# One weight block of the third projection taken into a decoder kernel's first rows, and an attention output computed turned, with the values as the stationary operand

## The chip, the cores and the metric

The program runs on one core of a Trainium2 chip. A core has five engines, each with its own queue of instructions: TensorE (PE, with its weight loads PEld), VectorE (DVE), ScalarE (ACT), GpSimd (POOL) and SyncE (SP). SP issues nearly all DMA transfers. The metric is the device time of one execution in microseconds (us), as the median of several runs; lower is better.

## The reference

Two decoder layers work on a sequence of 256 rows of 1024 features, all in float32. Cut to what matters:

```python
for i in range(2):
    h = rms_norm(x, norm_g[i])
    rq, rk, rv, rz, mq, mk, mv, mz = split(h @ w_in[i])      # eight groups of 512 columns
    r_out = silu(rz) * retention(rotary(rq), rotary(rk), rv, ret_norm_g[i])   # 4 heads of 128
    m_out = silu(mz) * softmax_attention(rms_norm(mq), rms_norm(mk), mv, rel_bias)   # 4 heads of 128
    x = x + concat([r_out, m_out]) @ w_out[i]
    gate = sigmoid(rms_norm(x) @ w_ple_gate[i])
    x = x + gate * rms_norm(p[i] @ w_ple[i], ple_norm_g[i])
```

With 256 rows the attention ("moba") has one block, so it is plain causal softmax attention with a bias per distance. Retention is linear attention with a decay by distance, followed by a normalisation per head.

## The kernel before

**Splitting floats.** TensorE multiplies in a reduced format (fp32r) at a quarter of the cost of full fp32 (in the profile 12 matmuls of 256 columns take 1.38 us, and 12 of 128 columns in full fp32 2.68 us). The kernel keeps full precision by splitting an operand into a high and a low part: ScalarE casts the high part, VectorE subtracts to get the low part, and three products (high x high, high x low, low x high) take the place of one. Weights come from memory through `wst` tiles (class `Stage`, 512 KB a chunk, two 128-row blocks k), are cast into `wh` (L350) and subtracted into `wl` (L353). `mm3` (L405 to L407) issues the three matmuls of 512 columns for one block k and one half m of the 256 rows. Small products are left in full fp32, which the profile shows as two records for one matmul.

**Order of the work in a layer.** The eight projections run in the order MQ, MK, RQ, RK, MZ, MV, RV, RZ (M for softmax attention, R for retention; Z are the gates). Then come the output projection, whose first half takes the softmax heads (k 4 to 7 of the tile `yT`) and whose second half takes the retention heads (k 0 to 3), the embedding product, and the gate product. Results of a projection leave PSUM through chains of operations on VectorE and ScalarE. Where a result is needed turned (features on partitions), `halves` (L621, ScalarE) sorts it into two 16-bit halves, `turned` sends it through a transposing DMA on SP's queue (L631), and VectorE copies the halves together (L640).

**First rows.** At the start nothing is on the chip. `first_rows` (L553) takes MQ's eight blocks one by one as they land; each block's transfer (`first_block`) brings 512 weight columns and 256 columns of the input. Blocks 0 and 1 of MK's weights (`key_block`, 256 KB each) lie behind blocks 0 and 1. The order in memory and on SP's queue is that of the dictionary `EARLY`.

**Attention.** `moba_scores` computes scores with query rows on partitions (L932, L950); `probs` adds the bias, takes the exponential and turns the result into the tile `PT` (keys on partitions; tile name PS in the profile). `moba_out` multiplies `PT` by the values `V` with the probabilities stationary (`pv`, L960, which retention's output uses too); `moba_y` multiplies by the gate and the reciprocal of the softmax sum (L978), turns the result and splits it into `yT` (`to_parts`, L657 and L659). Retention follows in `ret_scores_own` (L1010), `ret_scores` (L932), the decays `decayed` (L999), `ret_out` (L960), `ret_norm` and `ret_gate` (L1076). The tile `ST` of the retention scores takes the buffer of `PT`.

**What sets the order.** The program is laid out by a planner at build time (class `Flow`). Every chain of operations is a generator that asks for an engine with an estimated time, buffers to take and chains to wait for. The planner keeps a clock for each engine and gives the engine to the ready chain that is due first. What it lays down is a fixed order for each engine's queue. PE's order is that of the program text, but the small attention products stand in a list of groups, and `tick` puts one in between the matmuls of a projection once its inputs have been ready, by the planner's clock, for a margin.

Of the kernel before, what the change touches and what calls it, by code (L numbers as in the profile page):

```python
# [51 lines left out]
EARLY = {0: FIRST, "late": S, ("K", 0): GW, 1: BLOCK, ("K", 1): GW, **{k: BLOCK for k in range(2, KT)}}  # L52
# [3 lines left out]
LANES, LINE = 4, 4  # L56
TILE = 12 * ROW
HOP = 0.15
TURN = 0
AHEAD = 1.6  # L60
# [5 lines left out]
LIFT = {("gen", 38): 4.0, ("rope", 3): -7.0, ("gen", 4): -4.0, ("gate", 1): 1.0, ("hr1", 3): 2.0}  # L66
# [188 lines left out]
def tile_hybrid_trunk(ctx: ExitStack, tc: tile.TileContext, early, x, pT, ple_g, rel_bias,  # L255
# [243 lines left out]

    def key_half(src, hi, lo):  # L500
        yield ask(DVE, 0.35)
        nc.vector.tensor_copy(hi[:, S:], src[:, S:])
        firsts["K", 0, "lo"] = flow.begin(key_low(0, src, hi, lo), -19.6, flow.end + HOP)
# [52 lines left out]
    def first_blocks():  # L556
        home, at = act_p.tile([P, KT, 2, S], F32, name="a").rearrange("p k t s -> p (k t s)"), 0
        for k in range(KT):
# [6 lines left out]
            if k < 2:  # L565
                firsts["K", k] = flow.begin(key_block(k), k - 19.5, 0.0)
            at += BLOCK if k else 2 * FIRST
# [5 lines left out]
    for l in range(DEPTH):  # L573
# [3 lines left out]
        for g, half in pairs_in:  # L577
            skip = l == 0 and {MQ: 2, MK: 1 - half}.get(g, 0)
# [191 lines left out]
    def layer(l, aT):  # L770
# [92 lines left out]
        def value(g, m, ps):  # L863
            yield ask(ACT, 0.585, take=() if m else ("V",), after=need_stats(m) + ((VA[g],) if m else ()))
            if not m:
# [16 lines left out]
        def after_proj(g, m, ps):  # L882
# [4 lines left out]
            if g == RZ:  # L887
                YC[m, 0] = made(yT, m, 0, c)
# [22 lines left out]
        def probs(m, h0, per, ps):  # L911
# [16 lines left out]
            yield from turned(u, lambda: raw[:, :, h0:h0 + per, m * P:m * P + n])  # L928

        def three(ps, w, x):  # L930
            for i, (a, b) in enumerate(((0, 0), (0, 1), (1, 0))):
                nc.tensor.matmul(ps, w[a], x[b], start=i == 0, stop=i == 2)  # L932

        def moba_scores():
# [17 lines left out]
            for n in ("T", "T", "K2", "Q2"):  # L952
                flow.free(n, flow.clock[PE])

# [9 lines left out]
        yT, YC = Parts(), {}  # L964

        def moba_y(m, ps):
            ri = small(H, "ri")
            yield ask(DVE, 0.1)
# [3 lines left out]
            yield ask(DVE, 0.26, take=("tok",), after=(GC[MZ, m],))  # L972
            y = tok_p.tile([P, GW], F32, name="tok")
            for h in range(H):
                if h:
                    yield ask(DVE, 0.26)
                sl = slice(h * DH, (h + 1) * DH)
                nc.vector.scalar_tensor_tensor(y[:, sl], ps[:, sl], ri[:, h:h + 1], G[MZ][:, m, sl],  # L978
                                               op0=ALU.mult, op1=ALU.mult)
            flow.free("mix")  # L980
# [14 lines left out]
        SC, RO, RC = {}, {}, {}  # L995

        def decayed(h0, n, cols, ps):
            yield ask(DVE, 0.605, after=(L_DEC,))
# [4 lines left out]
        def ret_scores_own():  # L1003
            q, k = T[RQ], T[RK]
            flow.take("PS")
            box["ST"] = big.tile([P, H, S + P], F32, name="PS", bufs=1)
# [19 lines left out]
        def ret_norm(m, ps):  # L1026
# [23 lines left out]
            RO[m] = o  # L1050

        def ret_out():
            for m in range(MT):
                ps = pv(m, lambda h, m, b: box["ST"][:, h, S:] if b else box["ST"][:, h, m * P:(m + 1) * P], V[RV])
                RC[m] = flow.begin(ret_norm(m, ps), flow.soon(9.6))
# [257 lines left out]
```

## Time and profile before

| quantity | value |
|---|---|
| median of 3 runs | 296.58 us (296.27 to 297.05) |
| span of the profiled execution, first to last instruction | 294.1 us |
| median above that span | 2.48 us |
| PE busy | 288.9 us (98% of the span), 1411 matmul records |
| VectorE busy | 253.5 us (86%) |
| ScalarE busy | 214.7 us (73%) |
| GpSimd busy | 30.9 us (11%) |
| moved by DMA | 69.77 MB, mean 237 GB/s |

The page lists no separate whole time for the profiled execution; its span stands in the table, and the runs' times are longer by what lies around the span. The shares of busy time are averages over stages with different limits, so a change is read in its own stage. In a timeline row the columns are start, duration, engine, line, operation, output and inputs, and number of instructions; in brackets stands the engine's idle time before it and what ended it. Records of consecutive matmuls overlap, so the distance between starts is what one costs.

### The profile page before, as it was taken

To read this page: it belongs to the slowest core of one execution; us is meant where nothing else is said; L and a number is where in the kernel's file an instruction comes from. 1 tells how busy PE (TensorE), PEld (TensorE's weight loads), DVE (VectorE), ACT (ScalarE), POOL (GpSimd) and SP (SyncE) were. 2 spreads that over 40 slices of the span, in tenths; PEclk is the share of its full clock that TensorE was granted. 3 is DMA by queue.
4 is the path that set the end of the run, shared out by engine and by line. 5 is a ranking of instruction groups with operands and counts; after the bars stand their busy time and mean duration, and the time that the engine had idled before them with its cause. 6 is when DMAs were issued, how large, how long until landed. Compare 5 with 4: busy or idle time off the path is not lost.

```text
span 294.1 us, 4301 instructions
## 1 busy us (share of the span) xinstructions
PE 288.9 (98%) x1411; PEld 246.5 (84%) x1411; DVE 253.5 (86%) x461; ACT 214.7 (73%) x376; POOL 30.9 (11%) x44
## 2 busy tenths in 40 slices
PE   8999999999999999999999999999999999999994
PEld 4788888888899888888888888888898988888884
DVE  3967799999899999699999589999998797969942
ACT  3979974799747893998585896599646869479411
POOL 5004200000001200022003220000000030001300
PEclk9999999999999999999999999999999999999999
DMA  7999999998969868698689969787999766943021
GB/s 220 378 403 410 290 244 309 377 290 187 245 193 270 337 150 280 152 245 319 166 198 296 370 187 220 281 222 170 242 322 243 274 226 176 295 89 71 0 75 71
DMA packets 61774, 69.77 MB, mean 237 GB/s; under 512 B 46260, under 2 KB 47160, under 8 KB 61624
## 3 DMA queue, kind: packets, MB, share of 16 engines
q1 hardware_dynamic: 61712, 69.50, 79.7%
q8 instruction: 11, 0.18, 0.3%
q14 instruction: 11, 0.09, 0.1%
q0 software_dynamic: 32, 0.01, 0.0%
q10 hardware_dynamic: 8, 0.00, 0.0%
HBM read 57.42 MB, written 1.05 MB: 199 GB/s over the span
## 4 chain that ended last, share of the span: by engine, by line
PE 96%; DMA 2%; SPq 0%; ACT 0%; DVE 0%; issue 0%
PE acc L406 26%; PE acc L405 26%; PE acc L407 26%; PE acc L553 4%; PE mix L960 4%; PE mix L932 2%; DMA a<-in_early 2%; PE mix L407 1%; PE mix L743 1%; PE mix L742 1%; PE mix L406 1%; PE mix L744 1%; PE mix L405 1%; PE mix L1010 1%; PE mix L950 1%; ACT wh L459 0%
## 5 line engine op out<-in xcount | busy, mean ns | idle before, releaser
L405 PE MATMUL acc<-wh,a 128*128 128x512 f32 (+1 forms) x286 | 107.8, 377 | 0.0
L406 PE MATMUL acc<-wl,a 128*128 128x512 f32 (+1 forms) x286 | 107.7, 377 | 0.0
L407 PE MATMUL acc<-wh,a 128*128 128x512 f32 (+1 forms) x286 | 107.4, 376 | 0.0
L353 DVE TENSOR_TENSOR wl<-wst,wh 128x1024 fp32r<-128x1024 f32 x76 | 92.0, 1222 | 9.1 <-ACT wh L350 8.9
L350 ACT CAST wh<-wst 128x1024 fp32r<-128x1024 f32 x76 | 78.6, 1054 | 15.2 <-PE acc L407 6.0
L405 PEld LDWEIGHTS acc<-wh,a 128*128 128x128 f32 x286 | 53.5, 187 | 9.1
L407 PEld LDWEIGHTS acc<-wh,a 128*128 128x128 f32 x286 | 53.5, 187 | 9.0
L406 PEld LDWEIGHTS acc<-wl,a 128*128 128x128 f32 x286 | 53.5, 187 | 8.7
L621 ACT COPY u<-tok 128x1024 uint16<-128x1024 uint16 x30 | 31.1, 1053 | 12.7 <-DVE tok L978 7.9
L657 ACT CAST a<-tmp 128x512 fp32r<-128x512 f32 x20 | 12.4, 618 | 10.9 <-DVE tmp L654 8.3
L621 ACT COPY u<-x_t 128x1024 uint16<-128x1024 uint16 x12 | 12.5, 1042 | 10.2 <-DVE x_t L1138 6.8
L673 POOL TENSOR_TENSOR ro<-rs_t,neghalf 128x4 f32<-128x4 f32 x4 | 5.8, 1460 | 129.0 <-DVE rs_t L671 129.0
L640 DVE COPY tmp<-w 128x512 uint16<-128x512 uint16 x40 | 16.4, 466 | 0.1
L659 DVE TENSOR_TENSOR a<-tmp,a 128x512 fp32r<-128x512 f32 x20 | 13.7, 685 | 0.0
L640 DVE COPY T<-w 128x512 uint16<-128x512 uint16 x32 | 12.9, 467 | 0.7 <-DMA w<-u 0.7
L553 PE MATMUL acc<-wh,a 128*128 128x512 f32 (+1 forms) x42 | 11.3, 387 | 0.3 <-ACT wh L459 0.3
L960 PEld LDWEIGHTS mix<-V,PS 128*128 128x128 f32 x96 | 11.3, 192 | 0.3
L1189 DVE SCALAR_TENSOR_TENSOR tmp<-tmp,E 128x512 f32<-128x512 f32 (+1 forms) x9 | 5.7, 629 | 6.7 <-ACT tmp L1183 3.8
L960 PE MATMUL mix<-V,PS 128*128 128x128 f32 x96 | 11.4, 275 | 0.0
L1186 ACT ACTIVATE tmp<-acc,hr 128x512 f32<-128x512 f32 (+1 forms) x8 | 5.0, 631 | 8.5 <-PE acc L407 8.5
L405 PE MATMUL acc<-T,a 128*128 128x512 f32 (+1 forms) x30 | 11.0, 367 | 0.0
L407 PE MATMUL acc<-T,a 128*128 128x512 f32 (+1 forms) x30 | 10.9, 365 | 0.0
(144 smaller groups left out, 458.2 us busy)
## 6 DMA issues: line engine op xcount, KB each, us to landing
wst<-in_w_in SPq DMA_DIRECT2D x59, 512.0 KB, 6.3
wst<-in_w_out SPq DMA_DIRECT2D x16, 512.0 KB, 6.6
wst<-in_w_gate SPq DMA_DIRECT2D x16, 512.0 KB, 4.6
wst<-in_w_ple SPq DMA_DIRECT2D x4, 512.0 KB, 7.6
wst<-in_early SPq DMA_DIRECT2D x4, 384.0 KB, 7.4
a<-in_early SPq DMA_DIRECT2D x3, 384.0 KB, 5.8
x_t<-in_x SPq DMA_DIRECT2D x1, 1024.0 KB
gb<-in_ple_g SPq DMA_DIRECT2D x2, 512.0 KB, 6.7
```

Source lines behind the costliest of these rows:

```text
L350: nc.scalar.copy(hi, s)
L353: nc.vector.tensor_tensor(lo, s, hi.bitcast(F32), op=ALU.subtract)
L405: nc.tensor.matmul(ps, ah, wh, start=start, stop=False)
L406: nc.tensor.matmul(ps, ah, wl, start=False, stop=False)
L407: nc.tensor.matmul(ps, al, wh, start=False, stop=stop)
L553: nc.tensor.matmul(ps[m][:, sl], (a0.lo if which[0] == "lo" else a0.hi)[:, k, m * P:(m + 1) * P], columns(w, sl), start=start and i + j == ...
L621: nc.scalar.copy(u, src.bitcast(U16).rearrange("p (n t) -> p t n", t=2))
L640: nc.vector.tensor_copy(v, w[:, t].rearrange("p (h b) k -> p h (b k)", h=v.shape[1]))
L657: nc.scalar.copy(h, src)
L659: nc.vector.tensor_tensor(a.lo[:, k0:k0 + 4, m * P:(m + 1) * P], src, h.bitcast(F32), op=ALU.subtract)
L932: nc.tensor.matmul(ps, w[a], x[b], start=i == 0, stop=i == 2)
L960: nc.tensor.matmul(ps[:, h * DH:(h + 1) * DH], lhs(h, m, b), v[:, b, h * DH:(h + 1) * DH], start=b == 0, stop=b == m)
```

## The change

Two edits go together. The first takes block 0 of RQ's weights (the third projection) into the early transfers ahead of block 1, with its matmuls right after block 0 of MK, and block 1 of RQ's weights behind block 7, with its matmuls after block 6. RQ's own loop then leaves out these two blocks.

The second changes the softmax attention's output in both layers. The values are the stationary operand and the turned probabilities the moving one, so that the output comes with features on partitions. The probabilities over keys that both halves of the rows see, and the values of the first half of the keys, are split into high and low parts; for these three fp32r matmuls of 256 columns stand where one fp32 matmul per half stood. The rest (second half of the keys, second half of the rows) stays one fp32 matmul of 128 columns per head. The gate times the reciprocal is turned instead of the output (`gate_turned`), and lies in the part of `PT` that has been split already. The output is multiplied by it and split straight into `yT`. The parts of the probabilities lie in `yT`'s first half, those of the values in blocks 6 and 7 of `yT`, until `yT` is written. The retention scores take the buffer of `PT` only when the gates in it have been used, so the take stands on VectorE in `decayed`. Some planner constants change.

```diff
-EARLY = {0: FIRST, "late": S, ("K", 0): GW, 1: BLOCK, ("K", 1): GW, **{k: BLOCK for k in range(2, KT)}}
+EARLY = {0: FIRST, "late": S, ("K", 0): GW, ("R", 0): GW, 1: BLOCK, ("K", 1): GW, **{k: BLOCK for k in range(2, KT)}, ("R", 1): GW}
+THIRD = -19.3, -12.9
+GATES = 6.0
-LIFT = {("gen", 38): 4.0, ("rope", 3): -7.0, ("gen", 4): -4.0, ("gate", 1): 1.0, ("hr1", 3): 2.0}
+LIFT = {("gen", 38): 4.0, ("rope", 3): -7.0, ("gen", 4): -4.0, ("gate", 1): 1.0, ("hr1", 3): 2.0, ("rope", 2): 4.0}
...
+    def third_block(k):
+        yield ask(SP, 0.43, take=() if k else ("wst",), mb=0.25)
+        if not k:
+            firsts["R"] = wst_p.tile([P, 2, GW], F32, name="wst")
+        src = firsts["R"][:, k]
+        nc.sync.dma_start(src, early_block(("R", k)))
+        yield ask(ACT, 0.62, take=() if k else ("w",))
+        if not k:
+            firsts["Rw"] = wh_p.tile([P, 2, GW], F32R, name="wh"), wl_p.tile([P, 2, GW], F32R, name="wl")
+        hi, lo = firsts["R", k, "w"] = [v[:, k] for v in firsts["Rw"]]
+        nc.scalar.copy(hi, src)
+        firsts["R", k, "lo"] = flow.begin(key_low(k, src, hi, lo), THIRD[k] + 0.2, flow.end + HOP)
...
-            skip = l == 0 and {MQ: 2, MK: 1 - half}.get(g, 0)
+            skip = l == 0 and {MQ: 2, MK: 1 - half, RQ: 1 - half}.get(g, 0)
...
         def value(g, m, ps):
...
-            nc.scalar.activation(V[g][:, m], ps, AF.Copy, scale=stats(m)[0 if g == MV else 2])
+            if m or g == RV:
+                nc.scalar.activation(V[g][:, m], ps, AF.Copy, scale=scale)
+            else:
+                hi, lo = box["VT"] = [yT.both[:, k].rearrange("p t s -> p (t s)") for k in (6, 7)]
+                nc.scalar.activation(hi, ps, AF.Copy, scale=scale)
+                yield ask(DVE, 0.665)
+                nc.vector.scalar_tensor_tensor(lo, ps, scale, hi.bitcast(F32), op0=ALU.mult, op1=ALU.subtract)
...
         def probs(m, h0, per, ps):
...
+            src, hi, lo = (v[:, h0:h0 + per, m * P:(m + 1) * P] for v in (box["PT"], yT.hi, yT.lo))
+            yield ask(ACT, 0.1 + 0.11 * per)
+            nc.scalar.copy(hi, src)
+            yield ask(DVE, 0.08 + 0.13 * per)
+            nc.vector.tensor_tensor(lo, src, hi.bitcast(F32), op=ALU.subtract)
...
+        def turn_gates():
+            for m in range(MT):
+                if (MZ, m) in GC and (m, 2 * m) in PC and m not in GTC:
+                    GTC[m] = flow.begin(gate_turned(m), flow.soon(GATES))
+        def gate_turned(m):
             ri = small(H, "ri")
+            yield ask(DVE, 0.1, after=(GC[MZ, m], *PC.values()))
             nc.vector.reciprocal(ri, DEN[m])
             yield ask(DVE, 0.14)
             nc.vector.tensor_scalar(ri, ri, stats(m)[1], None, op0=ALU.mult)
-            yield ask(DVE, 0.26, take=("tok",), after=(GC[MZ, m],))
-            y = tok_p.tile([P, GW], F32, name="tok")
-            for h in range(H):
...
-                nc.vector.scalar_tensor_tensor(y[:, sl], ps[:, sl], ri[:, h:h + 1], G[MZ][:, m, sl],
-                                               op0=ALU.mult, op1=ALU.mult)
+            yield ask(DVE, 0.605, take=("tok",))
+            o = tok_p.tile([P, GW], F32, name="tok")
+            nc.vector.tensor_tensor(o.rearrange("p (h d) -> p h d", h=H), G[MZ][:, m].rearrange("p (h d) -> p h d", h=H),
+                                    ri[:, :, None].to_broadcast([P, H, DH]), op=ALU.mult)
...
-            u = yield from halves(y, "tok")
-            yield from to_parts(yT, m, 4, u)
+            u = yield from halves(o, "tok")
+            raw = box["PT"].bitcast(U16).rearrange("p h (k t) -> p t h k", t=2)
+            yield from turned(u, lambda: raw[:, :, :, m * P:(m + 1) * P])
+        def moba_y(i, ps):
+            yield ask(DVE, 0.605, take=("tmp",), after=tuple(GTC[m] for m in range(MT)))
+            t = tmp_p.tile([P, GW], F32, name="tmp").rearrange("p (h s) -> p h s", h=2)
+            nc.vector.tensor_tensor(t, ps.rearrange("p (h s) -> p h s", h=2), box["PT"][:, i::2, :S], op=ALU.mult)
+            flow.free("mix")
+            if i:
+                flow.free("PS")
+            yield ask(ACT, 0.53)
+            hi, lo = (v[:, H + i::2] for v in (yT.hi, yT.lo))
+            nc.scalar.copy(hi, t)
+            yield ask(DVE, 0.605)
+            nc.vector.tensor_tensor(lo, t, hi.bitcast(F32), op=ALU.subtract)
 
         def moba_out():
-            for m in range(MT):
-                ps = pv(m, lambda h, m, b: box["PT"][:, h, (m + b) * P:(m + b + 1) * P], V[MV])
-                YC[m, 4] = made(yT, m, 4, flow.begin(moba_y(m, ps), flow.soon(3.1)))
-            flow.free("PS", flow.clock[PE])
+            vh, vl = box["VT"]
+            banks = [bank(mix_p, "mix") for _ in range(2)]
+            for h0 in range(0, H, 2):
+                heads = [(h, slice(h * DH, (h + 1) * DH), banks[h - h0][:, h0 * P:h0 * P + S]) for h in range(h0, h0 + 2)]
+                for h, d, o in heads:
+                    flow.row(0.342)
+                    three(o, [v[:, d] for v in (vh, vl)], [v[:, h] for v in (yT.hi, yT.lo)], False)
+                for h, d, o in heads:
+                    flow.row(0.22)
+                    nc.tensor.matmul(o[:, P:], V[MV][:, 1, d], box["PT"][:, h, S:], start=False, stop=True)
...
         def decayed(h0, n, cols, ps):
-            yield ask(DVE, 0.605, after=(L_DEC,))
+            own = n == H
+            yield ask(DVE, 0.605, take=("PS",) if own else (), after=(L_DEC,) if own else (L_DEC, SC["own"]))
+            if own:
+                box["ST"] = big.tile([P, H, S + P], F32, name="PS", bufs=1)
...
         def ret_gate(g, m, ps):
...
-            while m not in RC:
-                yield ask(DVE, 0.0)
-            yield ask(DVE, 0.605, take=("tok",), after=(RC[m],))
+            yield ask(DVE, 0.605, take=("tok",), after=(RN[m],))
...
+            pr = [bank(mix_p, "mix") for _ in range(MT)]
             for k in range(KT):
                 first_rows(k, ps, k == 0, k == KT - 1)
                 if k < 2:
                     first_rows(k, pk, k == 0, False, ("K",))
+                if k in (0, 6):
+                    first_rows(k // 6, pr, k == 0, False, ("R",))
```

More of the change, by code (lines that the diff above doesn't have):

```diff
@@ L863, in value @@
         def value(g, m, ps):
-            yield ask(ACT, 0.585, take=() if m else ("V",), after=need_stats(m) + ((VA[g],) if m else ()))
-            if not m:
+            first = m == (g == MV)
+            yield ask(ACT, 0.585, take=("V",) if first else (),
+                      after=need_stats(m) + ((VA[g],) if m and g == RV else ()))
+            scale = stats(m)[0 if g == MV else 2]
+            if first:
                 V[g] = big.tile([P, MT, GW], F32, name="V", bufs=1)
                 flow.reach(VA[g])
-            nc.scalar.activation(V[g][:, m], ps, AF.Copy, scale=stats(m)[0 if g == MV else 2])
+            if m or g == RV:
[5 more added lines that the diff above has]
+                nc.vector.scalar_tensor_tensor(lo, ps, scale, hi.bitcast(F32), op0=ALU.mult, op1=ALU.subtract)
             flow.free("acc")
@@ L887, in after_proj @@
             if g == RZ:
-                YC[m, 0] = made(yT, m, 0, c)
+                made(yT, m, 0, c)
+            if g == MZ:
+                turn_gates()
         def project(gs, by_m=False, pre=None):
@@ L928, in probs, with three @@
             yield from turned(u, lambda: raw[:, :, h0:h0 + per, m * P:m * P + n])
-        def three(ps, w, x):
+            src, hi, lo = (v[:, h0:h0 + per, m * P:(m + 1) * P] for v in (box["PT"], yT.hi, yT.lo))
[3 more added lines that the diff above has]
+            nc.vector.tensor_tensor(lo, src, hi.bitcast(F32), op=ALU.subtract)
+        def three(ps, w, x, stop=True):
             for i, (a, b) in enumerate(((0, 0), (0, 1), (1, 0))):
-                nc.tensor.matmul(ps, w[a], x[b], start=i == 0, stop=i == 2)
+                nc.tensor.matmul(ps, w[a], x[b], start=i == 0, stop=stop and i == 2)
         def moba_scores():
@@ new lines, in gate_turned @@
+            raw = box["PT"].bitcast(U16).rearrange("p h (k t) -> p t h k", t=2)
[12 more added lines that the diff above has]
+            nc.vector.tensor_tensor(lo, t, hi.bitcast(F32), op=ALU.subtract)
+            flow.free("tmp")
@@ new lines, in moba_out @@
+        def moba_out():
+            vh, vl = box["VT"]
[8 more added lines that the diff above has]
+                    nc.tensor.matmul(o[:, P:], V[MV][:, 1, d], box["PT"][:, h, S:], start=False, stop=True)
+            for i, ps in enumerate(banks):
+                c = flow.begin(moba_y(i, ps), flow.soon(3.1))
+                for m in range(MT):
+                    for k in range(H + i, KT, 2):
+                        yT.made[m, k] = c
@@ L991, in moba_out @@
             flow.free("V", flow.clock[PE])
             ret_scores_own()
-        SC, RO, RC = {}, {}, {}
+        SC, RO, RN = {}, {}, [Mark() for _ in range(MT)]
         def decayed(h0, n, cols, ps):
-            yield ask(DVE, 0.605, after=(L_DEC,))
+            own = n == H
+            yield ask(DVE, 0.605, take=("PS",) if own else (), after=(L_DEC,) if own else (L_DEC, SC["own"]))
+            if own:
+                box["ST"] = big.tile([P, H, S + P], F32, name="PS", bufs=1)
             nc.vector.tensor_tensor(box["ST"][:, h0:h0 + n, cols], ps.rearrange("p (h t) -> p h t", h=n),
@@ L1117, in layer @@
                 load_p(l)
-            project((g,), by_m=g == RZ)
+            project((g,), by_m=g == RZ, pre={(RQ, m): pr[m] for m in range(MT)} if l == 0 and g == RQ else None)
         force_groups()
@@ L1285 @@
     early["late"] = sides[:, 1]
-    early |= {("K", k): w_in[0, MK, 0][:, k] for k in range(2)}
+    early |= {(n, k): w_in[0, g, 0][:, k] for n, g in (("K", MK), ("R", RQ)) for k in range(2)}
     w_gate = rows(a["w_ple_gate"], GW, 2)
```

18 lines of the change are left out of this document (8 added, 10 removed).

## The prediction

> **What bounds the kernel now.** I read the page's head and its chain that ended last, then TensorE's own waits, then the first ten microseconds instruction by instruction, then VectorE's share by stage.
>
> ```profile
> span 294.1 us, 4301 instructions
> PE 288.9 (98%) x1411; PEld 246.5 (84%) x1411; DVE 253.5 (86%) x461; ACT 214.7 (73%) x376; POOL 30.9 (11%) x44
> PE 96%; DMA 2%; SPq 0%; ACT 0%; DVE 0%; issue 0%
> ```
> ```profile
> PE acc L553 <- ACT wh L459: 0.3, 1, 0.3
> ```
>
> TensorE (PE) carries 96% of the chain that sets the end, and after the warm-up it has a single listed wait. A busy PE is not proof, because busy intervals overlap; so I checked the distance between starts, which a stall would stretch.
>
> ```profile
> 6.98 0.61 PE L553 MATMUL acc<-wl,a 128*128 128x512 f32 x2
> 7.92 0.72 PE L553 MATMUL acc<-wh,a 128*128 128x512 f32 x2 [0.33 <-ACT wh L459]
> 8.64 0.71 PE L553 MATMUL acc<-wl,a 128*128 128x512 f32 x2
> 9.20 1.50 PE L553 MATMUL acc<-wh,a 128*128 128x512 f32 x6
> 18.46 0.60 PE L553 MATMUL acc<-wh,a 128*128 128x512 f32 x2
> 18.91 0.38 PE L405 MATMUL acc<-wh,a 128*128 128x512 f32 x1
> ```
>
> From 9.20 to 18.91 there are 44 matmuls of 512 columns: 0.22 us each, no gap. Before 9.20 the same pitch shows what is lost: two matmuls from 6.98 should let the next start at 7.42 (it starts at 7.92, lost 0.50), two from 7.92 at 8.36 (8.64, lost 0.28), two from 8.64 at 9.08 (9.20, lost 0.12). So 0.90 us is lost around weight block 1, and from 9.20 on the kernel is a row of matmuls: the end moves by what leaves PE's work, by what fills those 0.90 us, and by any new stall.
>
> **Part one: block 0 of the third projection among the first rows.** Why PE loses time there:
>
> ```profile
> 5.52 0.29 DVE L502 CAST wh<-wst 128x256 fp32r<-128x256 f32 x1 [0.56 <-DMA wst<-in_early]
> 5.96 0.69 DVE L507 TENSOR_TENSOR wl<-wst,wh 128x512 fp32r<-128x512 f32 x1
> 7.25 0.62 ACT L459 CAST wh<-a 128x512 fp32r<-128x512 f32 x1 [1.32 <-DMA a<-in_early]
> 7.25 0.35 DVE L467 TENSOR_SCALAR a<-a 128x256 fp32r<-128x256 f32 x1 [0.59 <-DMA a<-in_early]
> 7.90 0.69 DVE L518 TENSOR_TENSOR wl<-a,wh 128x512 fp32r<-128x512 f32 x1 [0.30 <-ACT wh L459]
> 8.51 0.48 DVE L523 SCALAR_TENSOR_TENSOR a<-a 128x256 fp32r<-128x256 f32 x1
> ```
> ```profile
> 5.50:7.25 1.75, 1.75 (x9) 1.23 (x7) 0.99 (x3) 0.41 (x2) 1.44 (x5) 1.00 1.05 360
> 7.25:9.00 1.75, 1.41 (x6) 0.59 (x4) 1.45 (x4) 1.39 (x3) 0.32 (x2) 1.00 1.02 404
> ```
>
> Block 1 lands at about 7.2; ScalarE's cast, VectorE's low part and the low part of the input follow, and PE waits for each. The DMA columns (1.05 and 1.02 busy; 360 and 404 GB/s) say the transfers are saturated, so a transfer put ahead of block 1 delays everything behind it by its own length. The new block is 128 x 512 x 4 bytes = 0.262 MB: 0.65 us at 404 GB/s, 0.73 at 360.
>
> The new order, worked through: the second key-projection step still ends at 7.42. The new block lands near 5.5 + 1.15 = 6.65 (its 0.262 MB share of the 1.7 us that block 1's 0.393 MB takes after K0), its cast ends near 7.3 in ScalarE's idle 1.32 us, its low part on VectorE near 8.0. PE's six matmuls for it run from 7.42 to 8.74 without a wait. Block 1 lands 0.65 later, at 7.87; its low part comes 0.65 later too, so its last pair starts at 9.20 + 0.64 = 9.84. The six added matmuls take 6 x 0.22 = 1.32 us and are taken out of the later projection. Gain 1.32 - 0.64 = **0.68 us**. Bounds: no more than the 0.90 lost; at least 0.18, if block 1 is late by the slow 1.15 us. A loss would need block 1 1.32 us late, 0.262 MB at under 200 GB/s, beneath both rows.
>
> The Trainium skill, "DMA: Bandwidth & Descriptors", section Bandwidth, says that transfers from the main memory are bound by about 358 GB/s for a core; by it the block costs an estimated 0.73 us, the gain is 0.60 and the whole change 1.42. The row of 404 GB/s shows more than that rate here, so the measurement decides and 0.65 stays.
>
> The rest of the move costs nothing on the path. The SP queue gets one issue before block 1 and one behind block 7 where one 512 KB issue leaves; block 1 waits for bytes, not its issue. The loads of x, the constants and the later weights land some 1.3 us later (two blocks), while PE reaches the second projection 2 x 1.32 - 0.68 = 1.96 us later. The split of block 1 of the new weights falls where PE works through a backlog. The query and key heads are also 1.96 us later, and the scores with them; PE runs projections meanwhile.
>
> **Part two: the attention output turned, values stationary.**
>
> ```profile
> 79.46 2.68 PE mix L960 x24
> 82.14 0.89 PE mix L1010 x8
> 84.36 1.38 PE mix L932 x12
> ```
>
> Before, 12 products of full fp32 (two records each, 24) take 2.68 us a layer. After, each of 4 heads has three fp32r products of 256 columns (12 records, the form of L932: 1.38 us) and one fp32 product of 128 columns (8 records, the form of L1010: 0.89 us): 2.27. Saved 0.41 a layer, **0.82 us** in two. Bounds 0.7 to 0.9: all forms are in the trace.
>
> What is added lies on VectorE and ScalarE, which the chain does not hold (0% each) but which are nearly full in the attention stages.
>
> ```profile
> 49.40:79.40 30.00, 30.00 (x148) 25.81 (x147) 28.82 (x44) 24.71 (x42) 0.00 (x0) 1.00 0.97 285
> 187.00:217.00 30.00, 30.00 (x148) 25.80 (x147) 29.89 (x46) 25.49 (x42) 0.00 (x0) 1.00 0.83 225
> 3.83 0.41 ACT L480 CAST wh<-a 128x256 fp32r<-128x256 f32 x1
> 81.96 1.13 DVE L978 SCALAR_TENSOR_TENSOR tok<-mix,ri,G 128x128 f32<-128x128 f32 x4
> 109.81 0.68 DVE L659 TENSOR_TENSOR a<-tmp,a 128x512 fp32r<-128x512 f32 x1
> ```
>
> Per layer, by these rows: the split of the turned probabilities costs VectorE 0.68 + 2 x 0.48 = 1.64 and ScalarE 0.62 + 2 x 0.41 = 1.44; the low part of the values 0.68 more on VectorE; the output changes from 2 x 1.13 + 2 x 0.68 = 3.6 to six operations of 0.68 = 4.1. So VectorE gets 2.8 us, and some 3.7 us (gate times reciprocal and the turned copies) move ahead of the product. What hides it is the lead of the weight splits:
>
> ```profile
> 63.37 1.21 DVE L353 TENSOR_TENSOR wl<-wst,wh 128x1024 fp32r<-128x1024 f32 x1
> 68.74 0.38 PE L405 MATMUL acc<-wh,a 128*128 128x512 f32 x1
> 198.03 1.24 DVE L353 TENSOR_TENSOR wl<-wst,wh 128x1024 fp32r<-128x1024 f32 x1
> 202.80 0.38 PE L405 MATMUL acc<-wh,a 128*128 128x512 f32 x1
> ```
>
> Counting both rows in program order, the split ending at 64.58 is first used at 68.74 and that ending at 199.27 at 202.80: leads of 4.2 and 3.5 us, among the shortest of the two stretches, against 2.8 us more work spread over 30 us in which VectorE has 1.18 and 0.11 us idle. Cost nothing, if weights go first; with the cover gone, up to 1 us per layer.
>
> The second new wait is on the score buffer: the retention scores may overwrite it only when the turned gates in it are used.
>
> ```profile
> 76.03 0.82 DVE L640 COPY PS<-w 128x512 uint16<-128x512 uint16 x2 [0.83 <-DMA w<-u]
> 74.71 1.24 SPq L631 DMA_TRANSPOSE w<-u  x1
> DMA to landing us min/median/max: 3.0/3.2/5.4
> 83.12 1.05 ACT L621 COPY u<-tok 128x1024 uint16<-128x1024 uint16 x1 [2.58 <-DVE tok L978]
> 85.72 1.88 DVE L999 TENSOR_TENSOR PS<-mix,cst 128x512 f32<-128x512 f32 x3
> 89.57 2.84 PE L960 MATMUL mix<-V,PS 128*128 128x128 f32 x24
> 100.21 0.68 DVE L1076 TENSOR_TENSOR tok<-T,acc 128x512 f32<-128x512 f32 x1
> 110.74 0.38 PE L405 MATMUL acc<-K,a 128*128 128x512 f32 x1
> ```
>
> In layer 0 the last probabilities are copied by 76.85. Add 2.0 (later scores) and 0.9 (the split); the gates then take about 1.0 of VectorE (0.68 and an estimated 0.3 for two small ones), 1.05 of ScalarE, a turn of 3.2 from issue to landing (SPq's and the landing row), its copies of 0.8 and 1.24 of SP's second issue, with 0.4 for hops 7.7: ready near 87.5. The products with them end near 88.7, so the decays that began at 85.72 start some 3 us later and end near 90.6, and the retention output, at 89.57 before, moves to about 91. From it to the first gated multiply (100.21) lie 10.6 us, of which its own operations need 5 to 6. So it is hidden, by about 4 us. Queued behind the waiting multiply on VectorE are weight splits with the lead above.
>
> **The sum.** 0.68 + 0.82 = 1.50 off the profiled span: 294.1 to 292.6. The median of the runs, 296.58, lies 2.48 above that span, outside the program's instructions; I leave it alone: 296.58 - 1.50 = **295.1 us**. I take no deduction, since every added piece has a cover of some microseconds in its row. The tail after the last matmul does not change.
>
> **The rivals.** (A) Only the product gains: block 1 is late by the slow bound or more, or PE pays again behind it. For it: before 7.25 the first bytes come below 404 GB/s. Against it: the saturated rows. 296.58 - 0.82 = 295.8, within the noise.
>
> (B) VectorE becomes the bound for moments: 2.8 us a layer is more than the 1.18 and 0.11 us idle. The handovers are thin: in the rows above VectorE writes the first retention part of the output projection's input until 110.49, and PE uses it at 110.74, 0.25 us later. A delay of 0.4 to 0.5 us there in each layer takes 0.9 back: 296.0. Against it: that part follows its gate by 10 us, most of it with priority.
>
> (C) Slower: the retention chain in layer 0 comes late. Should the turned gates be ready later than 87.5 by more than the 4 us, then every further microsecond stalls PE at 110.74, where only 0.25 us is left. From 4 + 1.50 = 5.5 us on it decides, and at 6.5 us the time is 297.5. For it: the gates share SP's queue and both crowded engines with weight loads, and the new wait sits in front of three decays. A multiply that waits holds back what follows: in the rows of the first part VectorE stood idle for 0.30 us ahead of 7.90, though the subtraction of 8.51, behind it, had its input since 7.60. The Trainium skill, "TensorE: Matmul & The Clock Gate", section Part 1 (the architectural detail), says that the queues of VectorE and ScalarE are strictly first-in first-out; those 0.30 us agree. Against it: VectorE loses 1.6 us of other work after the product.
>
> **How the numbers follow.** Forecast (all of 1.50, within 0.4) 0.54; A 0.16, B 0.17, C 0.13. Runs before span 296.27 to 297.05, so about 0.3%, 0.9 us, is what a measurement can tell: faster means under 295.7. The forecast and a fifth of A give faster 0.57; the rest of A and B give same 0.30; C slower 0.13. The range runs from both upper ends (0.90 + 0.82 = 1.72, with 0.2 of scatter: 294.7) through A and B into the beginning of C: 296.9. The likeliest's own range is 294.7 to 295.5.
>
> **What would show it.** Right: PE's gaps between 7.4 and 9.2 shrink to about 0.2 us in all; the first rows end near 20.7; the product with stationary values takes 2.27 us a layer; PE's waits list nothing else. Wrong: a PE wait at L405 to L407 on VectorE or ScalarE near 60 to 115 or 190 to 255 (B), a PE wait at the output projection's retention part with decays started after 92 (C), or gaps of 0.5 us still standing before block 1 (A).

## The result, and the profile after

The changed kernel takes 300.5 us (median; 299.24 to 301.3 in six executions) against 296.58 us before (295.9 to 297.46 in the same session): ratio 1.0122, 95% interval 1.0101 to 1.0144. It is 3.9 us slower, and the forecast of 295.1 us was wrong in sign. The profiled execution took 301.3 us, its span is 299.3 us (before: 294.1). Ratios, here and below, leave out single executions over 1.5% above the fastest of the same kernel (one of e9 at 612.59 us, one of e17 at 300.82, one of the kernel before at 303.22), the medians do not.

The head of the page of the changed kernel, its chain that ended last, and TensorE's waits (what waited, for whom; us in total, times, longest):

```profile
span 299.3 us, 4289 instructions
PE 290.2 (97%) x1403; PEld 246.8 (82%) x1403; DVE 258.0 (86%) x462; ACT 217.4 (73%) x383; POOL 30.0 (10%) x44
PE 66%; DVE 15%; ACT 8%; issue 5%; DMA 5%; SPq 0%; ACTq 0%; DVEq 0%
```
```profile
PE acc L407 <- DVE tok L870: 2.8, 1, 2.8
PE mix L568 <- ACT wh L512: 1.1, 1, 1.1
PE mix L297 <- PEq L1371: 0.8, 1, 0.8
PE acc L409 <- DVE a L675: 0.2, 1, 0.2
```

PE held 96% of the chain and now holds 66%. VectorE is still "86% busy" and looks no fuller than before: the share over the whole span hides what happened, the waits show it. Wherever two starts of PE lie more than 0.26 us apart, what is beyond 0.22 us was summed: 3.29 us before (warm-up included) and 8.70 us after. These are 5.4 us more lost, against 0.8 saved by the product; the span grew by 5.2, and the remaining 0.6 lies in smaller distances and behind the last matmul.

Three places carry it. First the first rows (ScalarE, then PE):

```profile
5.13 0.41 ACT L500 CAST wh<-wst 128x256 fp32r<-128x256 f32 x1 [0.52 <-DMA wst<-in_early]
7.95 0.62 ACT L512 CAST wh<-wst 128x512 fp32r<-128x512 f32 x1 [2.41 <-DMA wst<-in_early]
...
6.93 0.61 PE L568 MATMUL acc<-wl,a 128*128 128x512 f32 x2
8.62 1.17 PE L568 MATMUL mix<-wh,a 128*128 128x512 f32 x4 [1.07 <-ACT wh L512]
...
10.96 1.26 PE L568 MATMUL acc<-wh,a 128*128 128x512 f32 x5
```

The third projection's block came at about 7.9, not 6.65, and PE, out of work at 7.38, waited for its cast. From 8.62 on little is lost: the ten matmuls up to 10.96 take 2.34 us where 2.20 would do. But block 1's last pair starts at 10.96 instead of 9.20: 1.76 us later for 1.32 us of added work. The first part lost 0.44 us where 0.68 was forecast as gain.

Second, in layer 0 (VectorE, then PE):

```profile
62.87 0.79 DVE L656 COPY T<-w 128x512 uint16<-128x512 uint16 x2 [1.83 <-DMA w<-u]
63.56 0.68 DVE L868 TENSOR_TENSOR tmp<-acc,cst 128x512 f32<-128x512 f32 x1
64.15 0.68 DVE L870 TENSOR_TENSOR tok<-acc,cst 128x512 f32<-128x512 f32 x1
...
61.67 0.38 PE L409 MATMUL acc<-wh,a 128*128 128x512 f32 x1
64.89 0.49 PE L407 MATMUL acc<-wh,a 128*128 128x512 f32 x1 [2.83 <-DVE tok L870]
66.28 0.63 PE L409 MATMUL acc<-wh,a 128*128 128x512 f32 x1
69.26 0.42 PE L407 MATMUL acc<-wh,a 128*128 128x512 f32 x1
```

VectorE stood idle for 1.83 us in front of copies whose turn had not landed. Behind them stood the rotation of the retention key heads, which reads the PSUM bank that PE's next projection needs: 3.0 us lost. Then the matmuls from 65.88 to 69.26 stand up to 0.43 us apart instead of 0.22, some 1.6 us more: the granted clock was 0.50 for 3.4 us, from 65.9 on. The place follows from the entry ("rope", 2) that the change adds to the hand-written table, a line that my prediction never costed. The second operation of that rotation before, and in e1 below, which is the changed kernel without the entry:

```profile
55.25 0.68 DVE L854 TENSOR_TENSOR tok<-acc,cst 128x512 f32<-128x512 f32 x1
57.46 0.68 DVE L870 TENSOR_TENSOR tok<-acc,cst 128x512 f32<-128x512 f32 x1
```

With the entry it comes at 64.15, behind the copies that wait; whether the entry alone would cost this in the kernel before was not run.

Third, the rest: 0.46 us at 139.6 (L409). The product itself did what was forecast; its rows in layer 0:

```profile
88.46 0.86 PE L964 MATMUL mix<-a 128*128 128x256 f32 x6
89.17 0.60 PE L1049 MATMUL mix<-PS,V 128*128 128x128 f32 x4
89.53 0.95 PE L964 MATMUL mix<-a 128*128 128x256 f32 x6
90.32 0.60 PE L1049 MATMUL mix<-PS,V 128*128 128x128 f32 x4
90.76 1.06 PE L1075 MATMUL mix<-T 128*128 128x128 f32 x8
```

From 88.46 to 90.76 it takes 2.30 us, against 2.68 before and 2.27 forecast.

### The profile page after: what moved, and what is told of

Read it like the earlier page. It is cut to its first block, busy times and chain, and to the rows that moved or that the text cites. A ratio compares the mean times of both kernels' runs of the same rounds, so it can differ in the third digit from the quotient of the medians.

```text
span 299.3 us, 4289 instructions
## 1 busy us (share of the span) xinstructions
PE 290.2 (97%) x1403; PEld 246.8 (82%) x1403; DVE 258.0 (86%) x462; ACT 217.4 (73%) x383; POOL 30.0 (10%) x44
## 4 chain that ended last, share of the span: by engine, by line
PE 66%; DVE 15%; ACT 8%; issue 5%; DMA 5%; SPq 0%; ACTq 0%; DVEq 0%
PE acc L409 19%; PE acc L407 19%; PE acc L408 18%; DVE wl L355 5%; PE acc L568 3%; DMA w<-u 3%; ACT wh L352 2%; DMA wst<-in_early 2%; PE mix L964 2%; ACT tmp L843 1%; ACT tmp L696 1%; DVE tmp L656 1%; DVE T L656 1%; DVE a L675 1%; ACT u L637 1%
## 5 line engine op out<-in xcount | busy, mean ns | idle before, releaser
L407 PE MATMUL acc<-wh,a 128*128 128x512 f32 (+1 forms) x294 | 111.7, 380 | 2.8 <-DVE tok L870 2.8
L409 PE MATMUL acc<-wh,a 128*128 128x512 f32 (+1 forms) x294 | 111.4, 379 | 0.0
L408 PE MATMUL acc<-wl,a 128*128 128x512 f32 (+1 forms) x294 | 111.2, 378 | 0.0
L407 PEld LDWEIGHTS acc<-wh,a 128*128 128x128 f32 x294 | 55.4, 189 | 12.3 <-DVE tok L870 3.2
L409 PEld LDWEIGHTS acc<-wh,a 128*128 128x128 f32 x294 | 55.4, 188 | 9.6
L673 ACT CAST a<-tmp 128x512 fp32r<-128x512 f32 x16 | 9.9, 621 | 7.1 <-DVE tmp L670 7.0
L656 DVE COPY tmp<-w 128x512 uint16<-128x512 uint16 x32 | 13.0, 463 | 0.8 <-DMA w<-u 0.7
L675 DVE TENSOR_TENSOR a<-tmp,a 128x512 fp32r<-128x512 f32 x16 | 11.0, 685 | 0.0
L568 PE MATMUL acc<-wh,a 128*128 128x512 f32 (+1 forms) x42 | 10.9, 374 | 0.0
L843 ACT ACTIVATE tmp<-acc 128x128 f32<-128x128 f32 x32 | 8.4, 287 | 2.3 <-PE acc L409 1.4
L696 ACT ACTIVATE tmp<-x_t 128x512 f32<-128x512 f32 x16 | 10.0, 638 | 0.0
L849 POOL TENSOR_TENSOR qr<-qms,neghalf 128x4 f32<-128x4 f32 x8 | 8.1, 1019 | 13.8 <-DVE qms L847 13.8
L407 PE MATMUL acc<-T,a 128*128 128x512 f32 x24 | 9.1, 381 | 0.0
```

The costliest lines, as they stand in the source:

```text
L407: nc.tensor.matmul(ps, ah, wh, start=start, stop=False)
L408: nc.tensor.matmul(ps, ah, wl, start=False, stop=False)
L409: nc.tensor.matmul(ps, al, wh, start=False, stop=stop)
L568: nc.tensor.matmul(ps[m][:, sl], (a0.lo if which[0] == "lo" else a0.hi)[:, k, m * P:(m + 1) * P], columns(w, sl), start=start and i + j == ...
L656: nc.vector.tensor_copy(v, w[:, t].rearrange("p (h b) k -> p h (b k)", h=v.shape[1]))
L673: nc.scalar.copy(h, src)
```

## The experiments

Two theories at the start. **Margin**: layer 0's retention chain (scores, decays, output, norm, gate, turn, output projection) had only the 0.25 us of rival B and C to spare, and either part of the change makes it late. **Lift**: the new table entry made the 3-us wait, and without it the change would win. Times are medians, ratios are against the kernel before in the same session.

**The lift, and each part alone.**

```
e1: after, -LIFT ("rope", 2): 4.0
e2: before + third_block and its first_rows
e3: before + turned product, no lift
```


> The changed kernel with one planner constant taken back: the entry that makes the first rope chain of the fourth projection (RK, rows 0 to 127) due 4 us later is left out; all arithmetic is the same. Theory 1 (that entry alone puts this chain behind copies that wait for a transposing DMA, so that PE waits about 3.0 us for the PSUM bank and then runs about 4 us at half clock, 1.8 us more): no PE wait of over 0.5 us after the first rows, granted clock 1.000, about 295.6 us. Theory 2 (VectorE has too much work in this stretch, and the wait comes back at another place whatever the order): a PE wait of 1 us or more remains between 55 and 120 us, about 298 us or more.

> The kernel before with the first part of the change alone: two weight blocks of the third projection among the first rows, attention output as before, planner constants as before. The prediction's step: gaps before weight block 1 shrink, gain 0.68 us (295.9). Theory 1 (the transfer of the new block lands at 7.9 instead of 6.65, so PE waits 1.2 us for it and the gap only moves): no gain, 296.2 to 297.0, with a PE gap of 1 us or more near 7.2 to 8.6.

> The kernel before with the second part alone: the attention output turned with the values stationary, without the two early blocks and without the new planner entry. The prediction's step: 0.4 us a layer off PE's work, no new stall: 295.8 us. Theory 2 (2.8 us more work a layer on VectorE makes PE wait): PE waits of more than 0.5 us in the attention or handover stages, 296.6 us or more.

e1 302.67 us, ratio 1.0205 (1.0176 to 1.0234); e2 298.25 us, 1.0056 (1.0043 to 1.0069); e3 298.88 us, 1.0101 (1.0067 to 1.0136). The lift theory fell: without the entry the wait at 61.7 is gone, and five others come, later and longer in all (e1, PE's waits):

```profile
PE acc L407 <- ACT a L673: 1.2, 1, 1.2
PE acc L409 <- DVE a L675: 1.1, 1, 1.1
PE acc L407 <- DVE tok L1140: 1.1, 1, 1.1
PE mix L993 <- DVE PS L1066: 1.0, 1, 1.0
...
PE mix L993 <- ACT tmp L1132: 0.8, 1, 0.8
```

The entry only chose where PE pays. In e2 the first rows gain nothing, and the handover fails (e2, PE and VectorE):

```profile
110.81 0.39 PE L408 MATMUL acc<-V,a 128*128 128x512 f32 x1
112.06 0.50 PE L406 MATMUL acc<-K,a 128*128 128x512 f32 x1 [0.86 <-ACT a L672]
113.15 0.49 PE L408 MATMUL acc<-K,a 128*128 128x512 f32 x1 [0.37 <-DVE a L674]
...
112.40 0.69 DVE L674 TENSOR_TENSOR a<-tmp,a 128x512 fp32r<-128x512 f32 x1
```

VectorE finishes the first retention part at 113.09 instead of 110.49. The scores' matmuls had come 1.56 us later (50.83 instead of 49.27); that was not absorbed in 60 us of stages but grew, and fell on the 0.25 us handover. In e3 (VectorE, then PE) the decays come late:

```profile
86.42 0.80 DVE L655 COPY PS<-w 128x512 uint16<-128x512 uint16 x2
87.70 0.79 DVE L655 COPY PS<-w 128x512 uint16<-128x512 uint16 x2
88.39 1.21 DVE L355 TENSOR_TENSOR wl<-wst,wh 128x1024 fp32r<-128x1024 f32 x1
89.52 1.28 DVE L1027 TENSOR_TENSOR tmp<-mix,PS 128x512 f32<-128x512 f32 x2
90.89 0.69 DVE L1065 TENSOR_TENSOR PS<-mix,cst 128x512 f32<-128x512 f32 x1
93.83 1.28 DVE L1065 TENSOR_TENSOR PS<-mix,cst 128x512 f32<-128x512 f32 x2
...
90.25 0.97 PE L963 MATMUL mix<-K,Q 128*128 128x256 f32 x6 [0.90 <-DVE tmp L1027]
94.67 3.00 PE L992 MATMUL mix<-V,PS 128*128 128x128 f32 x24 [2.09 <-ACT T L352]
```

The gates are copied by 88.5. The forecast of 87.5 holds 2.0 us for later scores, which e3 does not have; by the same sum it would be 85.5 here, so they are 3 us late. Their chain began at 79.58 where the sum has 77.75, and weight splits from 84.16 to 86.51 stand ahead of the copies. Decays follow at 90.89 and 93.83 (85.72 before), and the retention output at 94.67 waits for them though the row names a ScalarE cast. In the step between, the scores' second half waits 0.9 us for a PSUM bank that the product holds until the gates are there.

**The first rows.**

```
e4: before, early array 1024 columns wider
e7: e2, first_rows of ("R",) moved behind project((MK,))
e8: e2, third_block loads w_in[0, RQ, 0][:, k]; early array as before
```


> The kernel before, with 1024 columns that nobody reads added at the end of each of the 128 rows of the array of early blocks in memory, so that its rows lie 32,880 bytes apart as in the changed kernel instead of 28,784. Same instructions, same bytes moved. Theory A (the longer row distance slows the first transfers): between 4 and 9 us the DMA moves 250 to 330 GB/s instead of 350 to 410, block 1 lands 0.5 to 1 us later, 297.2 us or so. Theory B (the distance does not matter; the new block is late because it takes its turn behind and beside the others): 296.6 us, block 1 at 7.2 us.

> First part alone, but the early loaded block of the third projection is multiplied only after the second projection (where its matmuls stand in the kernel before) instead of among the first rows. Theory (the scores 1.97 us later pass through layer 0's retention chain to the output projection): the stalls of 1.02 and 0.53 us at 110.8 and 112.4 go, the early wait stays, 296.6 to 297.1 us. Rival (loading that block early is what costs, through the later loads): 298.2 as with the first part alone.

> First part alone, with the third projection's block loaded from the weights' own array, so that the early array keeps the row distance of before (28784 bytes instead of 32880). Theory R (the row distance spreads the 16 DMA engines): K's block lands at 5.5 again, the third's at about 6.7, block 1 at about 7.9, the first rows gain about 1 us over the first part alone: 297.2 us, with the handover's stall unchanged. Rival (the block comes late from the queue whatever the distance, or the engines' start spreads from run to run): first rows as with the first part alone, 298.2 us.

e4 296.88 us, 1.0009 (0.9995 to 1.0024): in its profile the key block and block 1 came 1.3 and 0.9 us later, but the median does not show it. e8 297.71 us, 1.0044 (1.0026 to 1.0063): 0.5 below e2, with the same losses of 1.03 and 0.53 us at the handover; the row distance may cost half a microsecond, the intervals overlap, and that stays open. e7 298.81 us, 1.0080 (1.0053 to 1.0107): the handover waits at 110 to 113 are gone, as the margin theory says, but the time is not: PE loses more in the first rows, which now have no added work, and 0.86 us in a later stage. So removing the late scores removes the handover wait; that the first part alone costs just this was too simple.

**The second part's layer.**

```
e5, e15: second part for l == 1 only
```


> Before, with the second part in layer 1 alone (layer 0 keeps the old product and gates). Theory (the new product itself saves about 0.4 us a layer of TensorE; what costs is layer 0's retention chain, which has no slack): no stall is added in layer 1, so 296.6 - 0.4 = 296.2 us, ratio 0.9986. Rival 1 (the turned product costs in either layer, through VectorE's added instructions or a throttled clock): 297 us or more. Rival 2 (the saving is no real saving, since other work just waits longer): 296.6.

> The version with the second part in layer 1 alone once more, for its interval: 296.2 us if TensorE's 0.4 us are saved whole, ratio 0.9986; 1.000 or above if they are not.

296.16 us, ratio 0.9982 (0.9961 to 1.0003), and again 296.85 us, 0.9998 (0.9980 to 1.0015). No wait is added in layer 1, where e5's product takes 2.30 us too, and the forecast 0.9986 lies in both intervals; so does no change. It is the best version tried, not one that is shown to beat the kernel before. What e3 loses is layer 0's. Why that layer: windows of the kernel before (columns: total, then busy us of PE, PEld, DVE, ACT, POOL, clock, DMA share, GB/s):

```profile
40.00:60.00 20.00, 20.00 (x102) 17.30 (x101) 19.93 (x31) 12.80 (x22) 0.00 (x0) 1.00 1.04 313
60.00:111.00 51.00, 51.00 (x267) 44.45 (x266) 48.69 (x95) 41.35 (x60) 2.92 (x2) 1.00 0.83 238
194.00:218.00 24.00, 24.00 (x114) 20.50 (x113) 23.84 (x37) 20.06 (x30) 0.00 (x0) 1.00 0.87 232
218.00:248.00 30.00, 30.00 (x169) 26.52 (x168) 25.03 (x58) 21.35 (x29) 2.92 (x2) 1.00 0.77 241
```

In layer 0 VectorE is busy 99.6% from 40 to 60 us and 95.5% from there up to the handover. Layer 1 is as full up to 218 us (99.3%; the prediction's row for 187 to 217 shows the same), but behind that it is 83% busy, and there lateness can be made good. In layer 0 two engines were full, not one. That this room is why layer 1 loses nothing is argued from these rows; no run took it away.

**Load or coupling?** Rival theories of the second part's loss: L, the splits' load on VectorE; C or G, the gates' chain (sums, scaling, turn, copies), which decays and PSUM banks now wait for.

```
e6: gates in a tile of their own, PS free after the product
e9: before + unused splits of P and V
e10: e3, product in whole fp32, no splits
e11: e3, layer 0's P subtractions on nc.gpsimd
e12: e6 + nc.scalar.copy(t, ps) frees the banks at once
e13: e6, gates without the sums
e14: e6, product in whole fp32, no splits
```


> Second part alone (no lift), but the turned gates go to a tile of their own instead of the probabilities' buffer, the gate's chain waits for the sums of the softmax alone, and the probabilities' buffer is given back when TensorE has read it. Theory A (the stalls of 0.96 and 2.26 us in layer 0 come from the decayed scores and their PSUM banks waiting for the turned gates): both stalls go, PV still starts some 3 us later than before (82 to 83 against 79.3), retention output at 91 to 92, some 0.5 to 1.2 us at the output projection's handover: 296.5 to 297.4 us. Rival B (VectorE and ScalarE load of the splits of P and V makes it late, whatever the buffers): the retention output stalls as before, 298.5 to 299.

> The kernel before, with the second part's splits added and not used: the same casts on ScalarE and subtractions on VectorE of the probabilities (three pairs a layer) and the subtraction for the values, at the same places; product, gates and buffers stay as before. Theory L (load: VectorE, busy 95% of layer 0's stretch from 70 to 111 us but 83% of layer 1's from 218 to 248 us, has no room in layer 0 for these 2.2 us): layer 0's retention chain comes 2 us later and TensorE loses 1 to 2.5 us at or before its output projection, layer 1 loses nothing: 297.6 to 299 us. Rival C (the coupling of decayed scores to the turned gates is what costs): 296.6 us, as before.

> Second part alone (no lift, gates turned into the probabilities' buffer as there), with the product in whole fp32 as before instead of three split products, so that the splits of the probabilities and values are not made; TensorE's product costs as before. Theory L (load of the splits): the stalls of 0.96 and 2.26 us in layer 0 mostly go, 296.6 to 297.3 us. Rival C (coupling): the retention output stalls by 2 us or more as with the splits, 298.5 to 299.3 us.

> Second part alone (no lift), with the three subtractions for the probabilities' low parts on GpSimd instead of VectorE in layer 0. Theory L: VectorE is relieved of 1.5 of the 2.8 us; if GpSimd takes about as long as VectorE for one (0.4 to 0.7 us), the stalls shrink by about half and the time is 297.3 to 298 us. If GpSimd takes 2 us or more for one, the product itself waits and the time stays at 298.9 or goes above. Rival C (coupling): 298.9 us whatever GpSimd takes, as long as the product does not wait for it.

> As the version with the gates in their own tile, and the product is copied from PSUM to SBUF by ScalarE at once (two copies of about 0.6 us a layer), so that its two banks come free without the gates. Theory G (the product's banks held until the gates are turned stop the retention scores' matmuls): the wait of 1.71 us at 87.2 goes, the retention output's wait shrinks, and only the load of the splits is left: 296.4 to 297.6 us. Rival L (VectorE's load is nearly all of it): 299 us or more.

> As the version with the gates in their own tile, but the gates' chain leaves out the softmax's sums (the product is not divided by them), so that it starts when the gate is projected, before the product. Theory G: the gates are turned before the product ends, banks come free at once, 296 to 297.4 us. Rival L: VectorE's work is nearly the same (four short instructions less), so 299 us or more.

> As the version with the gates in their own tile, with the product in whole fp32 (TensorE as before, no splits of probabilities and values, so some 2.2 us less on VectorE and about as much less on ScalarE a layer). Theory G: the wait for the turned gates stays, 298 to 299 us. Rival L: without the load no stall is left, 296.6 to 297 us.

e6 299.72 us, 1.0109 (1.0080 to 1.0138). e9 297.39, 1.0013 (0.9996 to 1.0031). e10 310.64: there the turned gates overwrite the probabilities ahead of the product, which waits 8.7 us for copies, so it bears on neither theory. e11 300.45, 1.0124 (1.0099 to 1.0148). e12 304.85, 1.0273 (1.0248 to 1.0297). e13 301.98, 1.0183 (1.0150 to 1.0215). e14 298.95, 1.0074 (1.0047 to 1.0100).

PE's waits of e6, of e9 and of e14, and GpSimd's rows in e11 (the second is two operations, of 0.74 and 3.55 us):

```profile
PE mix L965 <- DVE tmp L1040: 1.7, 1, 1.7
PE mix L994 <- DVE PS L1075: 1.1, 1, 1.1
```
```profile
PE mix L970 <- DVE PS L1009: 1.7, 1, 1.7
```
```profile
PE acc L409 <- DVE a L674: 1.0, 2, 0.8
...
PE mix L989 <- DVE PS L1069: 0.6, 1, 0.6
```
```profile
71.67 1.39 POOL L960 TENSOR_TENSOR a<-PS,a 128x512 fp32r<-128x512 f32 x1 [38.40 <-ACT a L957]
76.59 4.25 POOL L960 TENSOR_TENSOR a<-PS,a 128x256 fp32r<-128x256 f32 x2 [3.53 <-ACT a L957]
```

The splits alone, unused in the kernel before, already make the retention output wait 1.7 us for its decays (e9); in the median that costs 0.4 us, within what can't be told from nothing. Taking them out of e6 saves 0.8 us by the medians and 1.0 by the ratios (e14), though TensorE's 0.41 us a layer are given back there; without that it is 1.6 to 1.9. The intervals of e6 and e14 overlap, so the load shows in e9's wait more surely than in these times. It is not the whole: e14 without splits is still 0.74% slower than before. Taking the three subtractions off VectorE (e11) shortened the wait in the scores from 0.9 to 0.3 us, but the 2.1 us at the retention output stayed as in e3 and the time was no better; since GpSimd ended them only 0.4 us before the product began, this decides little. Giving the chain its own tile (e6), free banks (e12) or an early start (e13) did not bring the time back either; e12 and e13 were slower than e3, e6 the same within its interval. Each moves the written order on VectorE: in e12 the three decays begin at 90.22, 92.09 and 94.14 with other work between them, though the scores' matmuls had run at 87.26 without a wait for a bank. That fits a full VectorE and speaks against the banks; but why e12 and e13 also wait some 2 us in layer 1 was not followed up.

**Relief.** Work that has nothing to do with the change is taken from VectorE in that stretch:

```
Stage.plain (l == 0 and (g == RZ or g == RV and half == 1)): lo = hi, no subtraction
e16: on e3      e17: on e1      e18: on before
```


> Second part alone (no lift), and in layer 0 six weight subtractions of about 1.2 us on VectorE are left out (the low parts of the fourth value projection's second half and of the last gate projection; the high parts stand in their place, so those products are computed from high parts alone). Theory V (VectorE's row is full in layer 0 and the decayed scores stand in it behind other work): with about 7 us of it gone the waits of 0.96 and 2.26 us go, no handover wait comes, and both layers' 0.4 us are saved: 295.6 to 296.4 us. Rival G (the gates' chain of sums, scaling, turn and copies is too long in itself): at least 1.5 us of waits stay, 297.5 to 298.9 us.

> Both parts without the lift, with the same six subtractions left out in layer 0. Theory V: the five waits of 0.95 to 1.36 us between 94.9 and 118.1 us go but for the early one, and the clock stays whole: 296 to 297.5 us, against 302.7 with the subtractions. Rival G: 300 us or more.

> Control: the kernel before with the same six subtractions left out. TensorE has no wait there that they could remove, so 296.2 to 296.8 us by either theory; a gain of 1 us or more would mean that the relief shortens something else.

e16 297.68 us, 1.0047 (1.0024 to 1.0069); e17 297.92, 1.0051 (1.0023 to 1.0079); the control e18 297.72, 1.0041 (1.0023 to 1.0059). The control is over its range: in its profile PE loses less in gaps than before, but its matmuls stand 0.233 us apart from 8.3 to 50.7 us instead of 0.220, 2.4 us in all at a granted clock of 1.00, which the edit, at 77 us and later, does not explain. The profiles of e16 and e17 do not show it. So the control says little; against it e17 is level, against the kernel before it is still 0.2 to 0.8% slower. But 4.75 us of e1's 6 are gone with six subtractions of 1.2 us. PE's one wait behind the warm-up in e17:

```profile
PE mix L997 <- DVE PS L1070: 0.7, 1, 0.7
```

So with both parts in, a full VectorE made the late waits (theory V). e16 is level with the control by its median as well, but its profile does not go the same way. Its PE wait, and VectorE's rows:

```profile
PE mix L996 <- DVE PS L1069: 2.3, 1, 2.3
```
```profile
85.15 0.82 DVE L659 COPY PS<-w 128x512 uint16<-128x512 uint16 x2 [2.30 <-DMA w<-u]
86.39 0.81 DVE L659 COPY PS<-w 128x512 uint16<-128x512 uint16 x2 [0.42 <-DMA w<-u]
87.30 1.29 DVE L1031 TENSOR_TENSOR tmp<-mix,PS 128x512 f32<-128x512 f32 x2
88.70 0.69 DVE L1069 TENSOR_TENSOR PS<-mix,cst 128x512 f32<-128x512 f32 x1
```

Here VectorE has room and stands idle 2.7 us in front of the gates' turn; the decays still come at 88.70, three microseconds later than before, and PE still waits. That is theory G. By these two profiles both hold: the chain alone is late by some 2.3 us at the retention output, and VectorE's full row adds the rest when the scores are late as well. In the changed kernel itself PE, some 5 us behind by then, reaches the retention output at 97.09 without a wait, 0.3 us after the last decay. How the two theories add up there was not separated; the relief was not run with the entry in.

## Why the prediction was wrong, by its steps

- **The planner entry: never costed.** The sum took no deduction because "every added piece has a cover of some microseconds in its row"; the entry ("rope", 2) was not looked at. In the changed kernel the wait behind it and the halved clock after it are 4.6 us, the largest part of the miss. e1 shows that leaving it out does not win: the lateness is then paid elsewhere.
- **The block's landing (first part).** Forecast 6.65, measured 7.93, although the key block ahead of it was there at 5.11, earlier than before (5.50). The trace notes each landing in 16 steps: for this block 14 were done at 6.62, the last two at 7.86 and 7.92. In these 2.8 us the DMA moved 288 GB/s, three times the block's bytes, so later transfers went ahead while its last pieces were missing. Block 1 landed 1.68 us later, not 0.65. The sum took 360 and 404 GB/s, means of a stretch, for the landing of one block, while the cast waits for its last piece. Its bounds excluded a loss, and it lost 0.44 us. In e2 the piece that came late was the key block's (PE waited 1.3 us for its cast at L499). Why some pieces come late was not found.
- **"PE runs projections meanwhile": cost nothing.** Scores that come 1.96 us later (1.56 in e2) were said to be free; e2's handover shows 2.6 us at VectorE's end and 1.5 us lost by PE. The cover that I named, PE's own work, is not the cover of a chain that runs on VectorE; that was full from 40 us on, and the margin was the 0.25 us which I quoted under rivals B and C only.
- **VectorE's 2.8 us, hidden by the leads of the weight splits.** Mis-sized: the leads of 3.5 to 4.2 us are buffer for PE's next weights, and using them up delays all that is ordered behind. Costed at 0; e9 and e14 put the splits' part at 0.4 to 1.9 us, which is not clear of the noise.
- **The turned gates, "hidden by about 4 us".** The sum gives 85.5 for e3, without the late scores, and e3 measured 88.5: VectorE's other work delayed the start of the chain and its copies. What follows was late too: decays three microseconds later and a retention output at about 91, late scores included, became five and 94.67 in e3 without them, since the decays stand on VectorE behind the product's multiplies and weight splits and PE waits for them. And the 4 us were counted to the gated multiply, though PE itself waits at the retention output long before.
- **The product: 0.82 us.** Right: 2.30 us a layer measured, 0.38 saved in each, seen in e5's layer 1 as well.
- **Rival C had the mechanism of the single parts** (retention chain of layer 0 late) but set its threshold at 5.5 us and its place at the output projection; in the first part alone PE pays there for scores 1.56 us late. In the changed kernel the lift moved the place to 61.7, and the halved clock, of which no rival spoke, added 1.6 us. The terms of the profiled execution against the forecast: first rows 1.12, wait 2.99, clock 1.6, 139.6 0.46, product 0.06: 6.2 of the 6.7 us between a span of 292.6 and 299.3. The rest is not assigned. The 2.48 us that the forecast added to the span were too much by some 0.5: executions of the kernel before whose span is on record lie 1.9 to 2.0 us above it, so the traced one was a quick one.

## What to carry to other kernels

A profile whose chain is 96% one engine can hide a second engine that is just as full: look for the stretch in which another engine's row has no gap, and find the one thin handover at its end before costing a delay at nothing. The cover of a step is the slack on the engine on which its successors run, not the work of the bounding engine. When an ordering entry removes one wait, ask where the payment goes: with the lift and without it the same lateness was paid, in different places.

## What the hardware showed that I had not expected

- **The clock.** One wait of 2.83 us of PE was followed by half clock for 3.4 us. The changed kernel's executions show a granted clock of 0.991 to 0.994 in four of six (300.45 to 301.3 us) and 1.000 in two (299.24 and 299.83); a trace was kept of one of the six, so how long the wait was in the others is not known. The Trainium skill, "TensorE: Matmul & The Clock Gate", section Why this matters for your kernels, asks to avoid idle gaps above about 3 us because one idle window halves the clock. The measurements go below that figure: in e1 two waits of 0.79 and 0.96 us, ending at 96.1 and 97.7, were followed by half clock from 98.0 to 101.4, in e12 two of 1.44 and 1.28 by half clock from 95.5 to 98.9, while single waits of 2.27 us in e16's trace and 2.09 in e3's were not.
- **Landing.** The 16 steps in which a transfer lands can end far apart: e4's key block had 15 of them at 5.72 us and the last at 6.78.
- **GpSimd.** In e11 the two subtractions of 128 x 256 took 0.74 and 3.55 us there, against 0.41 each on VectorE in e3, and the one of 128 x 512 took 1.39 against 0.70. During the 3.55 us VectorE ran three operations with two inputs (1.21, 0.68 and 1.22 us); the other way round, a VectorE product of 128 x 512 that began at 71.82, during GpSimd's 1.39 us, took 1.79 us instead of 0.70. The Trainium skill, "SBUF — State Buffer", section SBUF: two separate sides, says that GpSimd and a VectorE operation with two inputs hold a shared port exclusively for a whole instruction; these durations agree with that, but no run here isolates it.
